# Hybrid encoder, two mixers: Ln/Exp in place of arithmetic roots and softplus, q left unnormalised, the out-projection in three fp32r products, and a new order with other PSUM pools

## The chip, the cores and the metric

The kernel runs on one core of a Trainium2 chip, in one launch. The metric is the device time of an execution in microseconds; the figure given for a kernel is the median of its runs.

## The reference

256 tokens of width 1024 go through two layers. Each layer is FFN, mixer, FFN, all with residuals; a final norm follows. Everything is fp32.

```python
for l in range(DEPTH):                                   # DEPTH = 2
    x = x + 0.5 * swiglu(rms_norm(x, ln_ffn1[l]), ffn1_w_in[l], ffn1_w_out[l])   # D_FF = 2752
    x = x + hybrid_mixer(rms_norm(x, ln_mix[l]), ...)
    x = x + 0.5 * swiglu(rms_norm(x, ln_ffn2[l]), ffn2_w_in[l], ffn2_w_out[l])
return rms_norm(x, ln_final)

def hybrid_mixer(h, ...):
    (wq, wk, wv, dq, dk, dv, dn_qkv, dn_z, dn_beta, dn_a) = split(h @ w_in)
    o_win = window_attention(...)        # 6 heads of 64, 2 kv heads, window 128, sink, ALiBi
    o_d = diff_attention(...)            # 4 heads: softmax(q0 k0) - lam * softmax(q1 k1), ALiBi
    o_diff = rms_norm(o_d, diff_g) * (1 - lam_init)
    qkv = silu(short_conv(dn_qkv, conv_w))               # width 5, 1152 channels
    q = l2_norm(q) * 64 ** -0.5;  k = l2_norm(k)         # rsqrt(sum of squares + EPS)
    beta = sigmoid(dn_beta);  g = -exp(a_log) * softplus(dn_a + dt_bias)
    o_c = gated_delta(q, k, v, beta, g) forwards + backwards   # chunks of 64, triangular solves
    o_dn = rms_norm(o_c, dn_g) * silu(dn_z)
    return concat([o_win, o_diff, o_dn]) @ w_out         # 1024 x 1024
```

## The kernel before

Activations are kept with channels on the 128 partitions: `x` is 128 x 8 x 256, eight channel blocks by 256 tokens. A weight comes as raw fp32 tiles of 128x1024, that is eight blocks of 128x128 (`fetch`, DMA from SP into a pool `rp` of eight buffers).

**The FFNs** multiply in three products. `load` (L243 to L254) makes two fp32r tiles of a raw one: a rounded copy `wh` on ScalarE (L252) and the remainder `wl` on VectorE (L253), both from a pool `wp` with four buffers each. The activations are split in the same way (`xh`, `xl` by `prep`, `hh`, `hl` in `hidden`). `mm3` (L256 to L260) then issues high x high, high x low and low x high for every weight block. 21 hidden blocks and a tail are computed, then eight output blocks. The scale of the norm (`norm_scale`: squares summed over channels with two small matmuls, then `rsqrt`) is applied after the product, in `hidden`, so an FFN starts before its norm is known. The squares are taken by `sq_add`: ScalarE squares a block, GpSimd adds (VectorE in the first FFN).

**The mixers** multiply in fp32: one `matmul` of the program on fp32 operands is two instructions on TensorE. The pieces of a mixer are issued in the order that `ORDER` lists by hand (a piece `name:args` is one call); the framework then schedules each engine's queue from its own model of times, with the place in the program as priority, so instructions can be hoisted over others that wait. The pieces that matter here:

- `A:*`, `N`, `V`, `G`: token projections, the norm, the values and the gates. `G` (`gates`) gets sigmoid and softplus by one Exp and a polynomial on VectorE (L464 to L474).
- `c:a:b`, `co`, `ce`, `qn:a`, `qc`: projection (`proj`, L427) and convolution of nine channel blocks, transposed to tokens; `qn` (`qk_norm`) takes the l2 norm of q (a = 0) and k (a = 1); `qc` transposes them back by chunk.
- `E`, `X`, `i`, `ir`, `im`, `io`, `ie`: decays, products of k and q, and the inverses of 24 triangular matrices, mostly by VectorE multiplies and reductions (`products`, L798 and L799).
- `p:*`, `d:h`, `h:h`, `w:b`, `hw:b`: attention projections, differential scores (`diff_scores`) with a merge of the two softmaxes on GpSimd (L728), window scores, and the heads' outputs.
- `f`, `g`, `sa`, `sb`, `sc`: the rest of the inverse and the scan over four chunks.
- `z`, `ze`, `on:p`: the output gate and the norm of the scan's output (`out_norm`).
- `oT`, `o:part:d`: the three results transposed into `oT`, and the out-projection (`out_proj`, L1047): part 0 uses the channel blocks 0 to 4, part 1 the blocks 5 to 7, eight output blocks each; part 1 ends with `prep` for the next FFN.

PSUM is three pools of banks: `pm` with two, `pd` with four, `pt` with two; `BANK` says which pool a result takes. `SHARED` names operations that go to GpSimd (with ScalarE's help where they start in PSUM). `rsqrt` starts from an integer estimate and takes three Newton steps, eleven VectorE instructions. The two ScalarE functions beyond copies and squares are Exp/Tanh in the mixers and Silu in the FFNs; a change of function table is an instruction on ScalarE (ACT_TABLE_LOAD).

Of the kernel before, what the change touches and what calls it, by code (L numbers as in the profile page):

```python
# [56 lines left out]
class Kernel:  # L57
# [104 lines left out]
    def rsqrt(self, v, n, name, out=None):  # L162

        nc, sp = self.nc, self.sp
        ti = sp.tile([P, n], I32, tag=f"rs_i{n}", name=f"{name}_i")
        nc.vector.tensor_scalar(ti, v.bitcast(I32), 1, None, ALU.arith_shift_right)
        y = sp.tile([P, n], F32, tag=f"rs_y{n}", name=f"{name}_y")
        nc.vector.tensor_scalar(y.bitcast(I32), ti, -1.0, float(0x5F3759DF), ALU.mult, ALU.add)
        a = sp.tile([P, n], F32, tag=f"rs_a{n}", name=f"{name}_a")
        for i in range(3):  # L170
            nc.vector.scalar_tensor_tensor(a, v, -0.5, y, ALU.mult, ALU.mult)
            nc.vector.tensor_tensor(a, a, y, ALU.mult)
            o = y if i < 2 or out is None else out
            nc.vector.scalar_tensor_tensor(o, a, 1.5, y, ALU.add, ALU.mult)
        return o
# [16 lines left out]
    def norm_scale(self, name, last=False):  # L192

        nc = self.nc
        ps = self.psum([P, 512], f"{name}_ps", "pt")
        for p in range(2):
            parts = [t for t in (self.sq, self.sq7) if t is not None]
            for t in parts:
                nc.tensor.matmul(
                    ps[:, p : p + 1], lhsT=t[:, p * P : (p + 1) * P], rhs=self.onec, start=t is parts[0], stop=t is parts[-1]  # L200
                )
# [1 line left out]
        nc.vector.tensor_scalar(v, ps[:, 0:2], 1.0 / D, EPS, ALU.mult, ALU.add)
        rt = self.sp.tile([P, 2], F32, tag="nr", name=f"{name}_r")
        self.rsqrt(v, 2, name, rt)
# [57 lines left out]
    def ffn(self, l, i, gnext, first):  # L263
# [3 lines left out]
        with tc.tile_pool(name=f"hp{nm}", bufs=1) as hp, tc.tile_pool(name=f"ht{nm}", bufs=3) as ht:  # L267
# [18 lines left out]
            late = []  # L286
            for j in range(NF):
# [13 lines left out]
                late.append((j, ps, pu))  # L301
                if j == 1:
                    if first is not None:
                        for k in range(KD):
# [4 lines left out]
                    nc.vector.tensor_scalar(rh, rb, 0.5, None, ALU.mult)
                if j >= 1:  # L310
                    for j_, pg, pu in late:
                        hidden(j_, pg[:, 0:S], pu[:, S : 2 * S], P, (0,))
                    late = []
# [40 lines left out]
    def mixer(self, l, gnext):  # L354
# [22 lines left out]
        with ExitStack() as ctx:  # L377
# [18 lines left out]
            oT = tile_([P, KD, S], "oT")  # L396
# [55 lines left out]
            def gates():  # L452
# [11 lines left out]
                z1 = tile_([P, 2, 24], "z1")  # L464
                ts(z1, ab, 2.0, None, ALU.add)
# [4 lines left out]
                sr = tile_([P, 2, 24], "sr")  # L470
                ts(sr, z2, 2.0 / 17, None, ALU.mult)
                for m in (15, 13, 11, 9, 7, 5, 3):
                    stt(sr, sr, 2.0 / m, z2, ALU.add, ALU.mult)
                stt(sr, sr, 2.0, z1, ALU.add, ALU.mult)  # L474
# [98 lines left out]
            def conv_end(a):  # L573
                if a < 2:
                    st["raw", a] = tile_([P, 2, 384], f"raw{a}", ("t4b", None)[a])
                for p in range(2):
                    act(st["raw", a][:, p, :] if a < 2 else vtok[:, p, :], st["tr", a][p][:, 0:384], AF.Copy)

            def qk_norm(a):

# [4 lines left out]
                nc.vector.tensor_reduce(ss, sqt.rearrange("p t (h d) -> p (t h) d", d=64), AX.X, ALU.add)  # L585
                ts(ss, ss, EPS, None, ALU.add)
                rq = self.rsqrt(ss, 12, f"{nm}qk{a}").rearrange("p (t h) -> p t h", t=2)
                if a == 0:
                    ts(rq, rq, 0.125, None, ALU.mult)
# [153 lines left out]
            def win_out(b):  # L743
# [6 lines left out]
                act(oT[:, b, :], pso[:, 0:S], AF.Copy)  # L750
# [276 lines left out]
            def out_norm(p):  # L1027
# [4 lines left out]
                ts(hv, hv, 1.0 / 64, EPS, ALU.mult, ALU.add)  # L1032
# [8 lines left out]
            def out_proj(part, d):  # L1041
                ks = ((0, 1, 2, 3, 4), (5, 6, 7))[part]
                ps = bank("py")
                for k in ks:
# [2 lines left out]
                    mm(ps[:, 0:S], lhsT=st["o", q // NBLK][:, c], rhs=oT[:, k, :], start=k == ks[0], stop=k == ks[-1])  # L1047
# [58 lines left out]
def build(tc, ins, out, phases=None):  # L1106
    with ExitStack() as ctx:
# [15 lines left out]
        for n, (w, l) in enumerate(order):  # L1123
# [5 lines left out]
            else:  # L1129
                K.ffn(l, int(w[3]), nxt, g(w, l) if n == 0 else None)  # L1130
# [128 lines left out]
```

## Time and profile before

| | |
|---|---|
| time, median of 3 runs | 1138.62 us (1137.33 to 1140.7) |
| the profiled execution | 1140.55 us, of which the trace's span is 1138.8 us |
| mean granted TensorE clock in it | 0.986 |
| FFN 1 of layer 0, from the start | to 198.4 us |
| mixer of layer 0 | 198.4 to 382.5 us |
| FFN 2 of layer 0 and FFN 1 of layer 1 | 382.5 to 755.0 us |
| mixer of layer 1 | 755.0 to 939.8 us |
| FFN 2 of layer 1 and the final norm | 939.8 to 1138.8 us |

Times in the profile are microseconds from the start of the span. PE is TensorE's matmuls, PEld its weight loads, DVE VectorE, ACT ScalarE, POOL GpSimd. A row of a group names line, engine, operation, output and inputs, shapes and count, then busy time and the mean of one in ns. A row of the timeline has start, duration (merged over xN instructions), and in brackets how long the engine sat idle before it and what ended that. A row of the windows has busy time and count for each engine, the granted TensorE clock (PEclk, 1.00 is full speed) and what the DMA moved. Matmuls overlap in the pipeline, so their pace is read from one start to the next and not from the duration of one.

### The profile page before, as it was taken

The page shows a single profiled execution, that of the slowest core. Times are in us where ns is not written, and L with a number is a line of the kernel's source. Part 1 is how long each engine was busy: PE and PEld are TensorE (multiplying, and loading weights), DVE is VectorE, ACT ScalarE, POOL GpSimd, SP SyncE. Part 2 cuts the span into 40 slices and gives each one's busy share as a digit, 9 for nine tenths or more (in the row PEclk, how much of TensorE's full clock was granted, in tenths as well). Part 3 has the DMA queues.
Part 4 walks back from the last instruction along what each step waited for, and adds up shares of the span by engine and source line. Part 5 has one row for each costly group of instructions (what it writes and reads, how often), then busy time and mean ns, then how long its engine had stood idle before and what let it go on. Part 6 is the DMA issues. An engine that isn't in the chain of part 4 may idle for free.

```text
span 1138.8 us, 21945 instructions
## 1 busy us (share of the span) xinstructions
PE 1103.7 (97%) x8970; PEld 1018.8 (89%) x8970; DVE 736.6 (65%) x1434; ACT 523.3 (46%) x967; POOL 75.6 (7%) x127
## 2 busy tenths in 40 slices
PE   7999999988999999999999999999999999999996
PEld 7999999776768999999999999988766789999996
DVE  6766754779847576666566666548796566666653
ACT  6544542263563454544444454424547345445441
POOL 0000011200102100000100000121010020000010
PEclk9999999998999999999999999999988999999998
DMA  8655653421214555565555565533211264556521
GB/s 315 223 185 185 201 182 122 148 93 56 72 42 131 191 178 186 185 200 181 177 182 182 179 201 184 170 121 121 92 56 37 76 204 151 183 184 204 185 94 38
DMA packets 49637, 173.64 MB, mean 152 GB/s; under 512 B 5504, under 2 KB 6784, under 8 KB 49536
## 3 DMA queue, kind: packets, MB, share of 16 engines
q1 hardware_dynamic: 49104, 171.64, 46.2%
q8 instruction: 70, 1.15, 0.4%
q10 hardware_dynamic: 432, 0.60, 0.2%
q14 instruction: 31, 0.25, 0.1%
HBM read 171.17 MB, written 1.05 MB: 151 GB/s over the span
## 4 chain that ended last, share of the span: by engine, by line
PE 80%; DVE 10%; issue 4%; ACT 4%; DMA 1%; POOL 1%; SPq 0%; DVEq 0%; ACTq 0%; POOLq 0%
PE ps L260 21%; PE ps L259 21%; PE ps L258 21%; PE py L1047 5%; PE pj L427 2%; DVE pad L549 2%; PE pz L438 2%; PE pv L438 1%; DVE pr L798 1%; DVE wl L253 1%; PE pso L749 1%; PE pss L712 1%; PE px L968 1%; DMA wr<-in_ffn 1%; DVE mxd L715 1%
## 5 line engine op out<-in xcount | busy, mean ns | idle before, releaser
L253 DVE TENSOR_TENSOR wl<-wr,wh 128x1024 fp32r<-128x1024 f32 x254 | 310.8, 1225 | 175.3 <-ACT wh L252 175.0
L252 ACT ACTIVATE wh<-wr 128x1024 fp32r<-128x1024 f32 x254 | 267.3, 1053 | 249.2 <-issue 143.2
L258 PE MATMUL ps<-xh,wh 128*128 128x256 f32 x1336 | 380.0, 284 | 1.1 <-ACT wh L252 1.1
L260 PE MATMUL ps<-xh,wl 128*128 128x256 f32 x1336 | 379.3, 284 | 0.8 <-DVE wl L253 0.8
L259 PE MATMUL ps<-xl,wh 128*128 128x256 f32 x1336 | 379.1, 284 | 0.0
L258 PEld LDWEIGHTS ps<-xh,wh 128*128 128x128 f32 x1336 | 257.2, 193 | 1.9 <-ACT wh L252 1.3
L260 PEld LDWEIGHTS ps<-xh,wl 128*128 128x128 f32 x1336 | 257.3, 193 | 1.2 <-DVE wl L253 1.2
L259 PEld LDWEIGHTS ps<-xl,wh 128*128 128x128 f32 x1336 | 257.4, 193 | 0.0
L260 PE MATMUL ps<-hh,wl 128*128 128x256 f32 x672 | 188.1, 280 | 0.0
L259 PE MATMUL ps<-hl,wh 128*128 128x256 f32 x672 | 187.9, 280 | 0.0
L258 PE MATMUL ps<-hh,wh 128*128 128x256 f32 x672 | 187.8, 279 | 0.0
L427 PE MATMUL pj<-xf,wr 128*128 128x256 f32 x544 | 130.1, 394 | 2.8 <-issue 2.8
L259 PEld LDWEIGHTS ps<-hl,wh 128*128 128x128 f32 x672 | 126.4, 188 | 0.0
L260 PEld LDWEIGHTS ps<-hh,wl 128*128 128x128 f32 x672 | 126.2, 188 | 0.0
L258 PEld LDWEIGHTS ps<-hh,wh 128*128 128x128 f32 x672 | 126.0, 187 | 0.0
L427 PEld LDWEIGHTS pj<-xf,wr 128*128 128x128 f32 x544 | 105.0, 198 | 19.0 <-issue 3.6
L190 POOL TENSOR_TENSOR sqacc<-sqacc,sqt 128x256 f32<-128x256 f32 x41 | 34.9, 851 | 733.5 <-ACT sqt L186 733.3
L281 ACT ACTIVATE hh<-h 128x256 fp32r<-128x256 f32 x88 | 36.1, 416 | 90.3 <-DVE h L279 90.3
L276 DVE TENSOR_TENSOR t<-ps,f_rb 128x256 f32<-128x256 f32 x88 | 36.8, 423 | 37.7 <-PE ps L260 37.5
L1047 PE MATMUL py<-oT,wr 128*128 128x256 f32 x256 | 57.8, 383 | 0.0
L282 DVE TENSOR_TENSOR hl<-h,hh 128x256 fp32r<-128x256 f32 x88 | 36.8, 423 | 30.5 <-ACT hh L281 30.5
L1047 PEld LDWEIGHTS py<-oT,wr 128*128 128x128 f32 x256 | 47.7, 190 | 6.8 <-DVE x L1054 0.3
(319 smaller groups left out, 1116.4 us busy)
## 6 DMA issues: line engine op xcount, KB each, us to landing
wr<-in_ffn SPq DMA_DIRECT2D x258, 512.0 KB, 3.5
wr<-in_mix SPq DMA_DIRECT2D x50, 512.0 KB, 3.5
wr<-in_mix SPq DMA_DIRECT2D x8, 408.0 KB, 3.1
wr<-in_mix SPq DMA_DIRECT2D x8, 384.0 KB, 3.0
x<-in_x SPq DMA_DIRECT2D x4, 256.0 KB, 4.8
ar<-in_ffn SPq DMA_DIRECT2D x8, 128.0 KB, 4.3
cb<-in_constb SPq DMA_DIRECT2D x1, 588.0 KB, 9.8
out_y<-fo SPq DMA_DIRECT2D x2, 256.0 KB, 2.4
```

The lines of the kernel that those rows point to most:

```text
L190: (eng or nc.gpsimd).tensor_tensor(self.sq, self.sq, t, ALU.add)
L252: nc.scalar.activation(h, w, AF.Copy)
L253: nc.vector.tensor_tensor(lo, w, h.bitcast(F32), ALU.subtract)
L258: mm(out, lhsT=ah, rhs=bh, start=start, stop=False)
L259: mm(out, lhsT=ah, rhs=bl, start=False, stop=False)
L260: mm(out, lhsT=al, rhs=bh, start=False, stop=stop)
L276: nc.vector.tensor_tensor(t[:rows], gate, rb[:rows], ALU.mult)
L281: nc.scalar.activation(hh[:n, j, :], h[:n], AF.Copy)
L282: nc.vector.tensor_tensor(hl[:n, j, :], h[:n], hh[:n, j, :].bitcast(F32), ALU.subtract)
L427: mm(ps[:, 0:S], lhsT=w[:, k * P : (k + 1) * P], rhs=xf[:, k, :], start=k == 0, stop=k == KD - 1)
L438: mm(st[name][p][:, 0:n], lhsT=xf[:, k, p * P : (p + 1) * P], rhs=w[:, c], start=k == 0, stop=k == KD - 1)
L1047: mm(ps[:, 0:S], lhsT=st["o", q // NBLK][:, c], rhs=oT[:, k, :], start=k == ks[0], stop=k == ks[-1])
```

## The change

- `rsqrt` takes Ln and Exp(-0.5 .) on ScalarE and one Newton step on VectorE in the mixers' norm, in `out_norm` and in the final norm (`log=True`); the FFNs' norms, k's norm and the differential norm keep the old form. softplus becomes Ln(1 + Exp(-abs)).
- `log_table` loads the table with Ln and Exp at three places: at a mixer's start, ahead of `on:1`, and in the last FFN.
- q is not normalised: its sum of squares is kept (`qe`), and goes in where `out_norm` had EPS.
- The out-projection multiplies with `mm3`: its weights go through `load` (8 tiles in each mixer), and the heads' outputs are written as `oh` and a remainder `ol` (5 blocks in the buffer of `xl`, 3 in that of k's raw tile).
- The squares for the FFN after a mixer are taken inside that FFN, with VectorE adds, after its second hidden block.
- The score tiles `pss` go from the pool `pm` to `pd`, `pw` from `pd` to `pt`. GpSimd gives up S2, t7 and x0, and gets x6. `ORDER` is changed.

```diff
-A:0 A:1 A:2 K N A:3 G V c:1:0 c:1:1 clear c:0:0 c:1:2 GS co:1:0 c:0:1 co:1:1 co:1:2 ce:1 GE GT E:1 qn:1 co:0:0 co:0:1
-c:0:2 co:0:2 ce:0 qn:0 E:0 E:3 qc:1:1 c:2:0 c:2:1 E:2 qc:0:0 qc:1:0 X:0:0 qc:0:1 ic X:1:1 X:0:1 X:1:0 i ir:1:2 ir:2:3
-ir:3:4 ir:4:5 ir:5:6 p:15 ir:6:7 ir:7:8 im:0 im:1 im:2 c:2:2 im:3 p:14 p:13 co:2:0 p:16 d:0 d:2 co:2:1 io:0 co:2:2 p:9
-d:1 p:12 d:3 w:0 io:1 h:2 h:1 p:10 h:0 io:2 io:3 h:3 p:11 w:1 w:2 hw:0 io:4 io:5 ie ce:2 dn hw:1 f g:0 hw:2 g:1 sa:0
-sb:0 oT:3:4 sc:0 sa:1 sb:1 sc:1 sa:2 sb:2 sc:2 sa:3 sc:3 z:0 z:1 z:2 z:3 ze on:1 o:0:0 on:0 o:0:1 o:0:2 o:0:3 o:0:4
-o:0:5 o:0:6 oT:7 oT:5:6 o:0:7 o:1:0 o:1:1 o:1:2 o:1:3 o:1:4 o:1:5 o:1:6 o:1:7
+lt A:0 A:1 A:2 K N A:3 G V c:1:0 c:1:1 c:0:0 c:0:2 c:1:2 clear GS co:1:0 c:0:1 co:1:1 co:1:2 ce:1 GE GT E:1 qn:1
+co:0:0 co:0:1 co:0:2 ce:0 qn:0 qc:1:1 E:0 E:3 qc:1:0 c:2:0 c:2:1 E:2 qc:0:0 qc:0:1 ic X:0:0 X:1:1 X:0:1 X:1:0 i ir:1:2
+ir:2:3 ir:3:4 ir:4:5 ir:5:6 p:15 ir:6:7 ir:7:8 im:0 im:1 im:2 c:2:2 p:14 p:13 co:2:0 p:16 d:0 d:2 co:2:1 co:2:2 im:3
+io:0 p:9 d:1 p:12 io:1 d:3 w:0 h:2 h:1 p:10 io:2 io:3 io:4 h:3 p:11 w:1 w:2 h:0 hw:0 io:5 ie ce:2 dn hw:1 f g:0 hw:2
+g:1 sa:0 sb:0 oT:3:4 sc:0 sa:1 sb:1 sc:1 sa:2 sc:2 sb:2 sa:3 sc:3 z:0 z:1 z:2 z:3 ze lt on:1 o:0:0 on:0 o:0:1 o:0:2
+o:0:3 o:0:4 oT:7 o:0:5 o:0:6 oT:5:6 o:0:7 o:1:0 o:1:1 o:1:2 o:1:3 o:1:4 o:1:5 o:1:6 o:1:7
...
-    pj="pm", pv="pd", pz="pm", py="pm", pss="pm", ..., po="pd", pw="pd", ...
+    pj="pm", pv="pd", pz="pm", py="pm", pss="pd", ..., po="pd", pw="pt", ...
-SHARED = set("O2 S2 d0 d1 d2 d3 g5 s3 t1 t7 t8 x0 x4 x5".split())
+SHARED = set("O2 d0 d1 d2 d3 g5 s3 t1 t8 x4 x5 x6".split())
...
@@ rsqrt
+        if log:
+            nc.scalar.activation(y, v, AF.Ln)
+            nc.scalar.activation(y, y, AF.Exp, scale=-0.5)
+        else:
...
+        steps = 1 if log else 3
+    def log_table(self):
+        self.tc.keep_in_program_order(self.nc.scalar.preload_act_table_set("natural_log_exp_and_others"))
...
@@ ffn
-                    if first is not None:
+                    if late:
                         for k in range(KD):
                             self.sq_add(k, nc.vector)
...
+            if gnext is None:
+                self.log_table()
...
@@ mixer
-            oT = tile_([P, KD, S], "oT")
+            oh = tile_([P, KD, S], "oh", None, F32R)
+            def ol(k):  # 0..4: buffer of xl; 5..7: buffer of raw1
...
+                if kind == "o":
+                    st[kind, i] = self.load(src, c0, n)
+                    return
...
@@ gates
-                z1 = tile_([P, 2, 24], "z1")
-                ts(z1, ab, 2.0, None, ALU.add)
...
-                for m in (15, 13, 11, 9, 7, 5, 3):
-                    stt(sr, sr, 2.0 / m, z2, ALU.add, ALU.mult)
-                stt(sr, sr, 2.0, z1, ALU.add, ALU.mult)
+                act(sr, ab, AF.Ln, bias=1.0)
...
@@ qk_norm
+                if a == 0:
+                    ts(ss, ss, EPS, 64 * EPS, ALU.add, ALU.mult)
+                    st["qe"] = ss.rearrange("p (t h) -> p t h", t=2)
+                    return
...
@@ win_out, to_oT
-                act(oT[:, b, :], pso[:, 0:S], AF.Copy)
+                act(oh[:, b, :], pso[:, 0:S], AF.Copy)
+                tt(ol(b), pso[:, 0:S], oh[:, b, :].bitcast(F32), ALU.subtract)
...
-                act(oT[:, k0, :], o_, AF.Copy, scale=g)
+                    act(oh[:, k, :], o_, AF.Copy, scale=g)
+                    stt(ol(k), o_, g, oh[:, k, :].bitcast(F32), ALU.mult, ALU.subtract)
...
@@ out_norm, out_proj
-                ts(hv, hv, 1.0 / 64, EPS, ALU.mult, ALU.add)
+                stt(hv, hv, 1.0 / 64, st["qe"][:, p, :], ALU.mult, ALU.add)
...
-                    mm(ps[:, 0:S], lhsT=st["o", q // NBLK][:, c], rhs=oT[:, k, :], start=k == ks[0], stop=k == ks[-1])
+                    wh, wl = st["o", q // NBLK]
+                    self.mm3(ps[:, 0:S], wh[:, c], wl[:, c], oh[:, k, :], ol(k), k == ks[0], k == ks[-1])
...
-                        self.prep(d, gnext)
+                        self.prep(d, gnext, False)
```

More of the change, by code (lines that the diff above doesn't have):

```diff
@@ L47 @@
 BANK = dict(
-    pj="pm", pv="pd", pz="pm", py="pm", pss="pm", pg="pt", pgr="pd", ptr="pd", pkq="pt", pe="pd", pq="pd", p1="pd",
-    p2="pt", pk="pd", px="pt", pS="pt", po="pd", pw="pd", pT="pd", pso="pd", pto="pd",
+    pj="pm", pv="pd", pz="pm", py="pm", pss="pd", pg="pt", pgr="pd", ptr="pd", pkq="pt", pe="pd", pq="pd", p1="pd",
+    p2="pt", pk="pd", px="pt", pS="pt", po="pd", pw="pt", pT="pd", pso="pd", pto="pd",
 )
-SHARED = set("O2 S2 d0 d1 d2 d3 g5 s3 t1 t7 t8 x0 x4 x5".split())
+SHARED = set("O2 d0 d1 d2 d3 g5 s3 t1 t8 x4 x5 x6".split())
 C_M0, C_M1, C_DD, C_WD, C_SEL = 0, 64, 128, 640, 1152
@@ L204, in norm_scale @@
         rt = self.sp.tile([P, 2], F32, tag="nr", name=f"{name}_r")
-        self.rsqrt(v, 2, name, rt)
+        self.rsqrt(v, 2, name, rt, log)
         pb = self.psum([P, 512], f"{name}_pb", "pt")
@@ L260, in mm3, with ffn @@
         mm(out, lhsT=al, rhs=bh, start=False, stop=stop)
-    def ffn(self, l, i, gnext, first):
+    def ffn(self, l, i, gnext, first, late=False):
         nc, tc = self.nc, self.tc
@@ L285, in ffn @@
                 self.start(first, hp, src)
-            late = []
+            wait = []
             for j in range(NF):
@@ L300, in ffn @@
                     self.mm3(o, w[g][0][:, c], w[g][1][:, c], self.xh[:, k, :], self.xl[:, k, :], k == 0, k == KD - 1)
-                late.append((j, ps, pu))
+                wait.append((j, ps, pu))
                 if j == 1:
-                    if first is not None:
+                    if late:
                         for k in range(KD):
@@ L310, in ffn @@
                 if j >= 1:
-                    for j_, pg, pu in late:
+                    for j_, pg, pu in wait:
                         hidden(j_, pg[:, 0:S], pu[:, S : 2 * S], P, (0,))
-                    late = []
+                    wait = []
                 if j == 3 and first is not None:
@@ L395, in mixer @@
             wq = tile_([P, 4, S], "wq")
-            oT = tile_([P, KD, S], "oT")
+            oh = tile_([P, KD, S], "oh", None, F32R)
+            low = {}
+            def ol(k):
+                i = int(k > 4)
+                if i not in low:
+                    low[i] = (
+                        mp.tile([P, 3, S], F32R, tag="raw1", name="olb") if i else
+                        self.xp.tile([P, KD, S], F32R, tag="xl", name="ola")
+                    )
+                return low[i][:, k - 5 * i, :]
             dqk = tile_([P, 2, 2, S], "dqk", "SC")
@@ L574, in conv_end @@
                 if a < 2:
-                    st["raw", a] = tile_([P, 2, 384], f"raw{a}", ("t4b", None)[a])
+                    st["raw", a] = tile_([P, 2, 384], f"raw{a}", ("t4b", "raw1")[a])
                 for p in range(2):
@@ L1129, in build @@
             else:
-                K.ffn(l, int(w[3]), nxt, g(w, l) if n == 0 else None)
+                K.ffn(l, int(w[3]), nxt, g(w, l) if n == 0 else None, n == 0 or order[n - 1][0] == "mix")
         K.final("fin")
```

33 lines of the change are left out of this document (13 added, 20 removed).

## Prediction

> **What bounds the kernel now.** I read the page's engine totals first, then windows by stage, then windows of 10 us inside a mixer, then the timelines where TensorE or VectorE stood idle. From the page:
>
> ```profile
> span 1138.8 us, 21945 instructions
> PE 1103.7 (97%) x8970; PEld 1018.8 (89%) x8970; DVE 736.6 (65%) x1434; ACT 523.3 (46%) x967; POOL 75.6 (7%) x127
> ...
> L253 DVE TENSOR_TENSOR wl<-wr,wh 128x1024 fp32r<-128x1024 f32 x254 | 310.8, 1225 | 175.3 <-ACT wh L252 175.0
> L252 ACT ACTIVATE wh<-wr 128x1024 fp32r<-128x1024 f32 x254 | 267.3, 1053 | 249.2 <-issue 143.2
> ...
> L276 DVE TENSOR_TENSOR t<-ps,f_rb 128x256 f32<-128x256 f32 x88 | 36.8, 423 | 37.7 <-PE ps L260 37.5
> ```
>
> 97% for PE looks like a matmul bound everywhere. The windows by stage say otherwise: the FFNs have no idle PE, the mixers some.
>
> ```profile
> 382.50:755.00 372.50, 372.30 (x3121) 371.89 (x3121) 231.19 (x336) 170.80 (x242) 13.05 (x15) 1.00 0.56 179
> 755.00:939.80 184.80, 177.43 (x1362) 135.79 (x1360) 131.97 (x355) 87.63 (x234) 24.30 (x39) 0.96 0.31 101
> ```
>
> Columns after the length: PE, PEld, DVE, ACT, POOL with counts, then the granted clock, DMA share, GB/s. A mixer is not one thing either. Windows inside the mixers:
>
> ```profile
> 278.40:288.40 10.00, 10.00 (x33) 6.67 (x32) 7.72 (x14) 4.39 (x16) 2.52 (x2) 0.74 0.17 54
> ...
> 825.00:835.00 10.00, 8.17 (x32) 4.79 (x30) 9.79 (x17) 3.82 (x14) 0.00 (x0) 0.91 0.22 70
> 835.00:845.00 10.00, 10.00 (x34) 7.05 (x34) 7.69 (x14) 4.16 (x13) 2.53 (x2) 0.75 0.18 53
> 845.00:855.00 10.00, 9.29 (x43) 6.64 (x42) 9.96 (x14) 5.06 (x18) 1.27 (x1) 0.93 0.20 54
> 855.00:865.00 10.00, 10.00 (x41) 8.27 (x40) 8.35 (x14) 5.02 (x17) 2.49 (x1) 0.73 0.08 24
> ...
> 915.00:925.00 10.00, 10.00 (x48) 8.80 (x48) 8.12 (x26) 4.22 (x6) 1.50 (x1) 1.00 0.63 194
> 925.00:935.00 10.00, 10.00 (x51) 8.86 (x50) 5.36 (x10) 4.55 (x10) 2.23 (x2) 1.00 0.87 303
> ```
>
> In the middle (inverse and scores) DVE is full at 9.79 and 9.96 of 10, and the TensorE clock is granted at 0.73 to 0.75 for stretches, in which DVE idles 2.28, 2.31 and 1.65 us. In the last third (915 to 935, the out-projection) PE is full at clock 1.00 and DVE and ACT are not: TensorE time saved there counts in full.
>
> **Out-projection.** Timelines of PE, and of the queue that feeds its second part:
>
> ```profile
> 183.12 0.28 PE L258 MATMUL ps<-hh,wh 128*128 128x256 f32 x1
> ...
> 190.54 0.28 PE L343 MATMUL ps<-hh,th 128*128 128x256 f32 x1
> ...
> 927.16 12.72 PE L1047 MATMUL py<-oT,wr 128*128 128x256 f32 x58
> ```
> ```profile
> 357.33 11.85 PE py L1047 x54
> 369.19 0.66 PE pto L411 x6
> ```
> ```profile
> 364.01 0.56 DVE L1036 TENSOR_TENSOR O<-zt,m0on_y 128x384 f32<-128x384 f32 x1
> ```
>
> A weight block costs two fp32 instructions, 2 x 12.72/58 = 0.438 us. In an FFN 63 fp32r matmuls start between 183.12 and 190.54, 0.118 us each, so `mm3` costs 0.353 us. 64 blocks x 0.085 = 5.4 us a mixer, 10.9 us in both. It adds, per mixer, 8 copies of 1.05 us on ACT and 8 remainders of 1.225 us on DVE, and 8 remainders of `ol` at about 0.42 us (row L276, same shape, from PSUM). Where they lie: four buffers of `wp` are free through the mixer, so four tiles can be split early; the other four follow in the out-projection, where today's four splits for the next FFN stand, and those move later, to the FFN's pace. DVE holds 13.5 us in the 20 us to 935; with 2 more splits (2.5) and three `ol` (1.3), less what `rsqrt` saves, it needs about 16 of 17 us. That fits narrowly, and the chain to part 1 narrows as well: the last normalised output ends at 364.57 and PE asks for it at 369.19, 4.6 us of slack. 27 blocks that are 0.085 shorter take 2.3, and `oT:5:6` now has one output of five blocks less ahead of it at issue, 1.8 if the schedule follows. Some 0.5 is left, 1 more from the shorter `rsqrt`; one extra split of 1.225 is covered, two are not. I charge 0.75 us per mixer (ends 0 and 2.5): 1.5.
>
> **Softplus, q and the norms.** The chain of waits, then the timelines:
>
> ```profile
> 211.33 0.20 DVE z L465
> ...
> 214.21 0.21 DVE sr L473
> ```
> ```profile
> 229.94 0.53 PE L411 MATMUL ptr<-cst,cs 128*128 128x128 f32 x2 [1.17 <-DVE cs L570]
> 249.45 0.84 PE L411 MATMUL pkq<-cst,raw 128*128 128x128 f32 x6 [0.89 <-DVE raw L592]
> 785.82 0.53 PE L411 MATMUL ptr<-cst,cs 128*128 128x128 f32 x2 [0.49 <-DVE cs L570]
> ```
> ```profile
> 244.49 0.17 DVE L166 TENSOR_SCALAR m0qk_i<-ss 128x12 int32<-128x12 int32 x1
> 248.47 0.17 DVE L589 TENSOR_SCALAR m0qk_y<-m0qk_y 128x12 f32<-128x12 f32 x1
> 248.75 1.02 DVE L592 TENSOR_TENSOR raw<-raw,m0qk_y 128x384 f32<-128x384 f32 x2
> ```
>
> The polynomial is 12 DVE steps in a row, 211.33 to 214.41; one Ln replaces it, so about 2.8 us of DVE and latency go. q's norm is 12 small steps strung from 244.49 to 248.64 (about 2.1 us of work, between others) and two multiplies, 1.02. PE is otherwise full in this stretch, so what can come back is what PE waited: 1.17 + 0.89 in layer 0, 0.49 + 0.89 in layer 1 (I take 0.89 there too, the k and q pieces being the same). Softplus addresses the first, q's norm the second: 3.4 us, and about 1 more since `qc:1:0`, k's, now stands ahead of `c:2:0` and leaves fewer copies in front of `X`. I take 4.0, ends 2 and 7.
>
> **The DVE-bound middle.** The list of waits and the timeline:
>
> ```profile
> PE pss L707 <- ACT sc L718: 3.0, 2, 1.5
> ```
> ```profile
> 831.47 0.38 PE L707 MATMUL pss<-ddb,sdiag 128*128 128x512 bf16 x1 [1.52 <-ACT sc L718]
> ```
>
> Once per mixer PE waits 1.5 us for a score bank, and within 2 us the clock falls (0.75 in 835 to 845), which starves DVE. With scores in four banks, and projections alone in `pm`, that wait should go. The DVE idle tied to low clock is 2.28 in layer 0 and 2.31 + 1.65 in layer 1, 6.2 in all; I take half, 3.1 (ends 0 and 6.2, plus PE time in the rival below). Against it: splits of the first out-projection tiles can be queued between the inverse's steps. Two per mixer would cost 4 x 1.225 = 4.9; I take half, 2.5, for those that fall into gaps (ends 0 and 9.8, all four early ones in the way). The order's moves (merges next to `io`, `im:3` later) I price at nothing: same instructions, and DVE has to execute all.
>
> **Tables, squares, the end.** ACT, then the chain of waits:
>
> ```profile
> 200.04 1.28 ACT L459 ACT_TABLE_LOAD   x1
> 201.34 0.21 ACT L459 ACTIVATE ea<-row 128x12 f32<-128x12 f32 x1
> ```
> ```profile
> 1128.88 0.18 DVE fin_i L166
> ...
> 1130.85 0.17 DVE fin_r L174
> ```
> ```profile
> 394.44 0.16 DVE L203 TENSOR_SCALAR f_v<-f_ps 128x2 f32<-128x2 f32 x1 [1.02 <-PE f_ps L199]
> ```
>
> A load costs 1.30 us from its start to the next ACT instruction. `lt` at a mixer's start takes the place of this one; I count one more for the first Tanh and one ahead of `on:1`, and one at the end: 5 x 1.3 = 6.5 us on ACT. It is more than half idle at the out-projection (4.22 and 4.55 of 10) and in a mixer as a whole (87.63 of 184.80), so nothing on the path; uncovered, 6.5. S2 and t7 come back from GpSimd to DVE, two steps of about the 0.51 that L592's take, where PE is full: nothing, at most 2 in both mixers.
>
> What ACT_TABLE_LOAD costs is also stated by the Trainium skill (ScalarE: Activation LUTs, section "What ACT_TABLE_LOAD costs"): 1283 ns and a drain of about 1380 ns, 2.66 us for a switch. The load's own 1.28 agrees; the drain does not show, ACT going on 0.02 us after it. By the page five loads are an estimated 13.3 us of ACT, which its idle time would still hold.
>
> Squares after a mixer: the FFN's norm scale is first read at 394.44, 12 us after the FFN began, and PE runs ahead meanwhile; eight squares and seven DVE adds (0.42 each) fit, cost nothing; if not covered 3 us each time, 6. The final `rsqrt` is bare at the end: 11 steps, 1128.88 to 1131.02, 2.1 us; two small ACT steps and three DVE steps at 0.2 each, with hand-overs, are 1.2. Gain 0.9.
>
> **Sum.** 10.9 - 1.5 + 4.0 + 3.1 - 2.5 + 0.9 = 14.9 us off the profiled execution's 1140.55 (span 1138.8 and 1.75 around it): 1125.6. The median shown, 1138.62, is 1.9 lower, so I predict 1123.7.
>
> **Rivals** (times at the level of the median; a change within 0.3%, 3.4 us, can hardly be told from none here).
>
> *Pool of four becomes the bound (slower).* `pd` now holds the pair `pss`, the pair `ptr` until `ce:2`, `pT`, `pso`: six wanted, four there. Each mixer has 7 score groups and 7 head outputs that can wait, on a PE queue that holds up all behind it. At 1.52 us each, as in the row above, 5 waits a mixer eat the gain; with one per score group, 7, it is 21.3 us in both mixers, and the time 1145. Against it: with two banks shared with projections, scores waited only once per mixer.
>
> *The splits sit in the inverse.* All four early ones delay DVE (9.8 in place of 2.5) and the clock stays as it is (minus 3.1): gain 4.5, 1134. For it: DVE is at 9.96. Against: ACT must copy first, and there are DVE gaps after 865 (8.35 of 10 and less).
>
> *The clock is no longer cut.* Low clock costs PE the missing share: in the quoted windows 2.6, 0.9, 2.5, 0.7 and 2.7 us, 9.4 together. If that and all the idle DVE time come back, 3.1 + 7 or so on top: 1113. For it: fewer PE gaps. Against: other gaps remain.
>
> On this the Trainium skill (TensorE: Matmul & The Clock Gate, "Part 1: The HAM clock gate", under "What's actually happening") says that the clock goes to half after at least one idle window of about 3.4 us. Here it falls after a gap of 1.52, so the trace disagrees. By that rule a wait of that length would have no hold on the clock, the 3.1 us in the sum would be nothing, and the time 1126.8.
>
> *It does not do what it says:* the fp32r pairs arrive too late and PE waits for each, so that the out-projection gains nothing: 1123.7 + 10.9 = 1135.
>
> **How the numbers follow.** Forecast 0.56, splits in the inverse 0.15, clock 0.16, pool of four 0.10, late pairs 0.03. Faster by over 0.3%: 0.56 + 0.16 and 0.10 of the 0.18 in the two weak gains, 0.82; within: 0.08; slower: 0.10. The forecast alone spans 1116 to 1132 from the ends above; to leave out two in ten the range takes in the weak gains above and most of the clock case below: 1111 to 1137.
>
> **What would show it.** Right: L1047's rows gone, L258 to L260 grown by 128 each, and out-projection windows at PE 10.00 that are some 5 us shorter; no `pss` wait on ACT sc; `pkq` not waiting for `raw`; a PEclk above 0.96 in the mixers. Wrong: PE rows of the out-projection waiting for `wl` or `ol`; `pss`, `pT` or `pso` waiting for ACT; DVE remainders L253 among L798 and L799; PE idle at the start of FFN 2.

## The result: 1138.0 to 1121.8 us, and the profile after

The kernel after takes 1121.82 us (median of 4, 1121.02 to 1122.8) against 1137.98 (median of 4) for the kernel before beside it: ratio 0.9852, 95% interval 0.9833 to 0.9871. The profiled execution took 1121.32 us. That of before, 1140.55, lies 2.6 us over its median, so the two profiles differ by more (19.3 us of span) than the medians (16.2). The page of after, and its windows by stage with the row that the prediction left out for before (columns as there):

```profile
span 1119.5 us, 22207 instructions
PE 1077.2 (96%) x9098; PEld 1009.7 (90%) x9098; DVE 751.0 (67%) x1374; ACT 545.4 (49%) x1006; POOL 60.1 (5%) x109
```
```profile
198.43:382.31 183.88, 174.62 (x1361) 133.24 (x1360) 133.69 (x355) 87.42 (x234) 24.32 (x47) 0.98 0.32 101
```
```profile
197.57:371.77 174.20, 161.39 (x1425) 128.56 (x1424) 137.01 (x322) 95.99 (x249) 18.47 (x40) 0.98 0.32 104
371.77:746.77 375.00, 374.69 (x3122) 374.32 (x3121) 234.86 (x345) 172.72 (x244) 11.50 (x13) 1.00 0.55 179
746.77:920.95 174.18, 161.70 (x1426) 128.74 (x1424) 136.90 (x322) 95.96 (x249) 18.10 (x32) 0.98 0.31 104
```

The mixers lost 9.7 and 10.6 us (183.9 and 184.8 to 174.2 and 174.2). The two FFNs between them, in which the change touches only where squares are taken, grew from 372.67 (382.31 to 754.98) to 375.00. A mixer is best cut at the first step after the inverses (`f`, the first `p<-WA`): before and after, layer 0.

```profile
328.33 1.61 PE L928 MATMUL p<-WA,XE 32*32 32x32 f32 x96
```
```profile
323.20 1.61 PE L955 MATMUL p<-WA,XE 32*32 32x32 f32 x96
```

From the mixer's start that is 129.9 and 125.6 us; from there to the FFN 54.0 and 48.6. So 4.3 us come from the part up to `f` and 5.4 from the part with the scan and the out-projection. What stands just ahead of `f` shows in the chain of waits (start, us, engine, tile and line), first of before, then of after:

```profile
305.47 0.41 ACT sc L698
...
317.86 2.20 PE pz L438 x6
...
321.67 2.58 PE pz L438 x8
...
325.26 2.13 PE pz L438 x6
```
```profile
309.80 1.14 DVE wl L265
...
311.10 0.68 ACT sc L723 x2
...
320.54 0.63 ACT hn L791
...
323.27 1.54 PE p L955 x94
```

Ahead of `f` the chain runs over ScalarE (window softmax, copies of heads and of the inverse's blocks) in both kernels, from 305.5 and from 311.1. In before its last 10 us, from 317.9, lie on PE, with 6.9 us of the output gate's projection `pz`; after, these have run earlier. The windows say the same: ahead of `f` ScalarE is full for 20 us, in the last ten of them PE is nearly full too in before (9.74), and VectorE is not.

```profile
297.60:307.60 10.00, 8.70 (x44) 7.19 (x44) 9.94 (x17) 5.90 (x22) 2.54 (x1) 1.00 0.17 52
307.60:317.60 10.00, 8.50 (x49) 6.37 (x49) 6.42 (x16) 9.87 (x24) 0.00 (x0) 1.00 0.17 52
317.60:327.60 10.00, 9.74 (x40) 5.18 (x42) 3.81 (x17) 9.10 (x27) 0.00 (x0) 1.00 0.05 9
```
```profile
307.60:317.60 10.00, 9.23 (x48) 6.30 (x49) 6.45 (x21) 9.89 (x34) 0.00 (x0) 1.00 0.44 159
317.60:327.60 10.00, 9.38 (x187) 6.02 (x187) 5.00 (x20) 9.13 (x17) 0.00 (x0) 1.00 0.35 109
357.60:367.60 10.00, 8.64 (x71) 8.18 (x70) 8.38 (x14) 6.35 (x13) 1.44 (x3) 1.00 0.47 154
283.50:290.30 6.80, 4.09 (x13) 3.11 (x14) 6.80 (x10) 3.86 (x10) 1.26 (x1) 0.50 0.28 77
```

The first fence is before, the second after. Its last two rows: in the out-projection PE is at 8.64 of 10, no longer full, and the clock is still halved once a mixer. The waits of after (us in all, times, longest), and three of the four early splits, on VectorE:

```profile
PE pss L699 <- DVE c L748: 11.3, 2, 5.8
...
PE py L270 <- DVE x L1082: 1.8, 4, 0.6
```
```profile
284.45 1.22 DVE L265 TENSOR_TENSOR wl<-wr,wh 128x1024 fp32r<-128x1024 f32 x1
...
290.33 1.21 DVE L265 TENSOR_TENSOR wl<-wr,wh 128x1024 fp32r<-128x1024 f32 x1
...
292.89 1.21 DVE L265 TENSOR_TENSOR wl<-wr,wh 128x1024 fp32r<-128x1024 f32 x1
```

The score wait on ScalarE is gone; in its place PE waits up to 5.8 us once a mixer for VectorE. As far as VectorE bounds this stretch, the wait costs nothing itself: VectorE is busy for 5.74 of its 5.77 us, and for 6.80 of 6.80 in the halved stretch that begins inside it.

### The profile page after: what moved, and what is told of

It is laid out like the page before. It is cut to its first block, busy times and chain, and to the rows that moved or that the text cites. A ratio compares the mean times of both kernels' runs of the same rounds, so it can differ in the third digit from the quotient of the medians.

```text
span 1119.5 us, 22207 instructions
## 1 busy us (share of the span) xinstructions
PE 1077.2 (96%) x9098; PEld 1009.7 (90%) x9098; DVE 751.0 (67%) x1374; ACT 545.4 (49%) x1006; POOL 60.1 (5%) x109
## 4 chain that ended last, share of the span: by engine, by line
PE 78%; DVE 13%; ACT 4%; issue 3%; DMA 1%; POOL 1%; DVEq 0%; SPq 0%; ACTq 0%
PE ps L272 21%; PE ps L270 21%; PE ps L271 21%; PE pj L455 4%; PE pv L466 2%; DVE pr L825 2%; DVE wl L265 2%; PE py L270 1%; DVE pp L826 1%; PE py L271 1%; PE py L272 1%; DVE pad L568 1%; ACT wh L264 1%; DVE mxd L740 1%; PE px L995 1%
## 5 line engine op out<-in xcount | busy, mean ns | idle before, releaser
L265 DVE TENSOR_TENSOR wl<-wr,wh 128x1024 fp32r<-128x1024 f32 x270 | 330.5, 1226 | 167.6 <-ACT wh L264 167.1
L264 ACT ACTIVATE wh<-wr 128x1024 fp32r<-128x1024 f32 x270 | 284.2, 1054 | 243.9 <-issue 153.0
L270 PE MATMUL ps<-hh,wh 128*128 128x256 f32 x672 | 190.2, 283 | 0.0
L270 PEld LDWEIGHTS ps<-hh,wh 128*128 128x128 f32 x672 | 129.0, 192 | 0.0
L271 PEld LDWEIGHTS ps<-hl,wh 128*128 128x128 f32 x672 | 129.0, 192 | 0.0
L272 PEld LDWEIGHTS ps<-hh,wl 128*128 128x128 f32 x672 | 129.0, 192 | 0.0
L455 PEld LDWEIGHTS pj<-xf,wr 128*128 128x128 f32 x544 | 101.7, 193 | 18.3 <-issue 3.9
L198 POOL TENSOR_TENSOR sqacc<-sqacc,sqt 128x256 f32<-128x256 f32 x27 | 24.5, 907 | 741.6 <-ACT sqt L194 741.6
L194 ACT ACTIVATE sqt<-x 128x256 f32<-128x256 f32 x49 | 19.8, 409 | 56.3 <-DVE x L361 52.5
L568 DVE SCALAR_TENSOR_TENSOR pad<-pad,cwh 128x256 f32<-128x256 f32 x68 | 33.1, 487 | 12.1 <-ACT pad L562 6.8
```

What stands on the lines that cost most here:

```text
L198: (eng or nc.gpsimd).tensor_tensor(self.sq, self.sq, t, ALU.add)
L264: nc.scalar.activation(h, w, AF.Copy)
L265: nc.vector.tensor_tensor(lo, w, h.bitcast(F32), ALU.subtract)
L270: mm(out, lhsT=ah, rhs=bh, start=start, stop=False)
L271: mm(out, lhsT=ah, rhs=bl, start=False, stop=False)
L272: mm(out, lhsT=al, rhs=bh, start=False, stop=stop)
```

## The experiments

Medians against the kernel before on the same chip (1138.0 to 1139.1 us). "To `f`" and "to the FFN" are the two parts of a mixer in the profiled execution, the second up to the FFN's first product behind the last one of the out-projection.

| kernel | us | ratio, 95% interval | layer 0: to `f`, to the FFN | layer 1 |
|---|---|---|---|---|
| before | | 1 | 129.9, 54.0 | 130.8, 54.0 |
| before + split out-projection | 1146.08 | 1.0053 (1.0034 to 1.0071) | 132.2, 52.7 | 134.6, 53.5 |
| the same + short root, squares moved | 1140.54 | 1.0008 (0.9997 to 1.0019) | 131.4, 50.8 | 134.7, 51.9 |
| before + order and pools | 1128.55 | 0.9910 (0.9893 to 0.9926) | 123.9, 53.1 | 124.7, 52.9 |
| after | 1121.82 | 0.9852 (0.9833 to 0.9871) | 125.6, 48.6 | 125.7, 48.5 |
| after, out-projection in fp32 | 1127.04 | 0.9890 (0.9867 to 0.9914) | 124.0, 52.8 | 124.7, 52.7 |
| after, squares back | 1125.25 | 0.9872 (0.9854 to 0.9889) | 125.8, 49.7 | 124.9, 49.8 |
| after, polynomial and q's norm back | 1135.67 | 0.9951 (0.9929 to 0.9972) | 127.1, 55.3 | 125.9, 55.3 |
| after, pools back | 1144.84 | 1.0053 (1.0033 to 1.0074) | 134.8, 51.5 | 133.4, 51.5 |

**The split out-projection, alone and taken out**

```diff
 # before, with
+st["o", i] = self.load(src, c0, n)
+self.mm3(ps[:, 0:S], wh[:, c], wl[:, c], oh[:, k, :], ol(k), k == ks[0], k == ks[-1])
 # after, with
-self.mm3(...)
+mm(ps[:, 0:S], lhsT=st["o", q // NBLK][:, c], rhs=oT[:, k, :], ...)
```

> The kernel before with one part of the change alone: the out-projection in three fp32r products (weights through load, heads' outputs as oh and a remainder ol). Order, pools, softplus, roots and q stay as before. Theory A (the parts add up): 64 blocks a mixer at 0.353 in place of 0.438 us are 5.4 us a mixer, and the stretch from the last px to the FFN shrinks from 27.1 to about 21.6 us in each mixer; time about 10 us under before (0.991). Rival B (the gain needs the other parts: without the new order and the shorter rsqrt the split tiles and ol come late, or the splits sit in the inverse): PE waits for wl or ol in the out-projection, or the inverse ends later, and the time is less than 5 us under before (over 0.9956).

> The kernel after with the out-projection taken back to fp32 (raw weights, oT), all else as after. Theory A: 5.4 us a mixer come back at the out-projection, and the splits no longer lie among the inverse's steps, so what is lost is 10.8 us less what these cost (3 x 1.22 a mixer at most): 4 to 11 us over after, 1126 to 1133. Rival B (splits in the inverse cost as much as they bring, and the gain of the change is in the rest): within 3 us of after.

Alone, it makes the kernel slower; rival B held by its time and by the later inverse (the waits for `wl` or `ol` that it named did not come). Windows of its mixers and its longest wait of PE in the out-projection, then the mixer and `f` of after in fp32:

```profile
196.33:381.18 184.85, 174.62 (x1428) 134.90 (x1426) 142.31 (x369) 94.30 (x242) 23.36 (x47) 0.97 0.30 98
754.42:942.46 188.04, 177.87 (x1427) 136.99 (x1426) 141.92 (x369) 94.19 (x242) 23.21 (x39) 0.95 0.31 96
```
```profile
PE py L258 <- DVE x L1071: 5.2, 6, 1.3
```
```profile
197.23:374.04 176.81, 166.14 (x1362) 128.95 (x1360) 128.42 (x311) 89.90 (x242) 17.62 (x40) 0.98 0.33 105
```
```profile
321.22 1.61 PE L940 MATMUL p<-WA,XE 32*32 32x32 f32 x96
```

In before's order the splits push `f` back by 2.3 and 3.8 us, and PE then waits for VectorE's sums into `x` (5.2 us in both mixers), so that only 1.3 and 0.5 of the 5.4 us a mixer come through. In after the same edit is worth 5.2 us: `f` comes 1.6 and 1.0 us later, and the part behind it is 4.2 us shorter in each mixer. Theory A held there.

**Two parts that make room at the end**

```diff
 # before + split out-projection, with
+r = self.rsqrt(hv, 6, f"{nm}on{p}", log=True)     # lt ahead of on:1
+self.prep(d, gnext, False)                        # squares inside the FFN
 # after, with
-self.prep(d, gnext, False)
+self.prep(d, gnext)
```

> The kernel before with the split out-projection, and two more parts of the change: the rsqrt of out_norm by Ln and Exp with one Newton step (with the table load ahead of on:1), and the squares after a mixer taken inside the FFN. 64 unused bytes keep hh and hl at the addresses of before. The split alone measured 1146.1 us, 7 over before: off1 came 2.3 and 3.8 us later in the mixers, and the stretch from the last px to the FFN stayed at 27 us although the products are 5.4 us shorter. Theory A (the end of a mixer is bound by the chain of small VectorE steps to oT:5:6 and by ScalarE and VectorE work on x, xh, squares and splits, so that shorter products pay only with these taken out): the stretch falls to 22 us or less, 5 us a mixer under the split alone, about 1136, and off1 stays as late as in the split alone. Rival B (the split weights themselves come late, by DMA or for want of buffers): the stretch stays at 26 us or more, time about 1145.

> The kernel after with the squares after a mixer back at the mixer's end (eight ScalarE squares of 0.40 us between the xh, adds on GpSimd), all else as after. Theory A: in the split out-projection's end ScalarE then has 3.2 us more among the xh and the splits of the next FFN, PE waits, and 2 to 3 us a mixer are lost: 1126 to 1128. Rival B (ScalarE has room, as the prediction had it for the move): within 1.5 us of after, 1121.8.

With both parts added to the split alone, the stretch from the last px to the FFN fell from 27 to 25.1 us, not to 22: A only by half, B wrong. The time is that of before. The squares alone, put back into after, cost 3.4 us, just under what A had and twice what B allowed.

**Order and pools**

```diff
 # before, with the new ORDER (without lt), BANK and SHARED
 # after, with
-pss="pd", pw="pt"
+pss="pm", pw="pd"
```

> The kernel before with the new order, the new pools (pss in pd, pw in pt) and the new list of GpSimd's operations, and nothing else of the change (fp32 out-projection, polynomial, q normalised, Newton roots, squares at the mixer's end). Alone, the split out-projection was 7 us slower than before; taking the pools out of after cost 23 us, the early arithmetic 14, the split 5. Theory A (order and pools are what makes the room: they take out the score waits, after which the clock is cut and VectorE starves, and let z and the out-projection run under the inverse): off1 earlier than 129.9 by 2 us or more per mixer, 4 to 8 us under before, 1131 to 1135. Rival B (each part only pays with the others; with VectorE as full as in before, the order gives nothing): within 3.4 us of before, 1136 to 1142.

> The kernel after with the pools back (pss in pm, pw in pd), the new order and all else as after. Theory A (the middle is bound by VectorE; where the scores wait matters little): last window score later, off1 within 1 us of after, time within 2 us of after, 1120 to 1124. Rival B (the score waits and the clock cut behind them held VectorE, the prediction's 3.1 us): off1 1.5 us later or more in each mixer, time 1125 or more.

Order and pools (with the new list of GpSimd's operations, which was not run apart) alone bring 10 us, more than A had it. A's mechanism is not what shows, though: PE's wait for a score bank, 1.5 us in before, stays.

```profile
PE pss L707 <- ACT sc L718: 2.9, 2, 1.4
```

Only the halved clock behind it is shorter: the granted clock of layer 0 is 0.90 and 0.93 in the two windows of 10 us from 267.6, where before has 0.96 and 0.70. With the new pools the wait is gone only where VectorE's early work is gone as well (after, and after in fp32); with the polynomial and q's norm back in after it is 1.5 us again, with the old pools 1.8. The mixers of this run, a stretch ahead of `f`, and `f`; then the last window scores in before, here, and in after with the pools back:

```profile
198.45:375.51 177.06, 166.38 (x1362) 128.00 (x1360) 132.03 (x357) 86.59 (x233) 22.50 (x45) 0.99 0.33 105
748.26:925.87 177.61, 167.75 (x1362) 129.14 (x1360) 131.81 (x357) 86.95 (x233) 22.18 (x37) 0.98 0.33 105
```
```profile
297.60:307.60 10.00, 9.77 (x53) 6.70 (x53) 9.45 (x21) 8.94 (x23) 0.01 (x1) 1.00 0.33 105
```
```profile
322.39 1.61 PE L928 MATMUL p<-WA,XE 32*32 32x32 f32 x96
```
```profile
313.90 1.66 PE L674 MATMUL pss<-wq 64*128 64x256 f32 x8
```
```profile
303.70 1.14 PE L674 MATMUL pss<-wq 64*128 64x256 f32 x8
```
```profile
319.35 1.13 PE L699 MATMUL pss<-wq 64*128 64x256 f32 x4
```

The last window scores come 10 us earlier, ScalarE's softmax work is taken up earlier (8.94 of 10 in the window from 297.6, where before has 5.90), and `f` comes 6 us earlier. That each follows from the one before it is read from the traces; no run holds the scores back alone. With the pools back, the new order is worse than the old, and B held by more than it asked: `f` is 9.2 and 7.7 us later than in after. PE waits 1.61 us for VectorE and, 5 us on, 1.66 for a score bank, and a stretch of 13.7 us at half clock lies there, in which VectorE is busy for 9.81 only.

```profile
269.40 0.38 PE L732 MATMUL pss<-ddb,sdiag 128*128 128x512 bf16 x1 [1.61 <-DVE dqk L686]
...
274.48 0.58 PE L732 MATMUL pss<-ddb,sdiag 128*128 128x512 bf16 x1 [1.66 <-ACT sc L743]
```
```profile
269.70:283.40 13.70, 11.62 (x29) 7.16 (x29) 9.81 (x15) 5.53 (x20) 1.26 (x1) 0.50 0.00 1
```

So the new order needs the pools; whether they would bring as much in the old order was not run.

**Softplus and q**

```diff
 # after, with
-act(sr, ab, AF.Ln, bias=1.0)
+...                                   # the polynomial
-if a == 0: st["qe"] = ...; return     # q's sum of squares kept
+rq = self.rsqrt(ss, 12, ..., log=False); ts(rq, rq, 0.125, ...); two multiplies
```

> The kernel after with the polynomial for softplus and the normalisation of q (rsqrt in three Newton steps, two multiplies) back, out_norm with EPS; order, pools, split out-projection and out_norm's Ln and Exp as after. Theory A (all VectorE work ahead of the inverse delays it one for one, since VectorE is full from there to off1): about 2.8 us of polynomial and 3.1 us of q's norm come back on VectorE, pq and off1 come 3 to 5 us later in each mixer, time 6 to 10 us over after, 1128 to 1132. Rival B (only PE's own waits come back, as the prediction counted, 4.0 in both mixers): about 1125.8, off1 later by 2 us a mixer.

Both theories missed the place. The inverse starts 2.4 us later in both mixers (first multiply `pr` 61.8 us into the mixer, 59.4 in after), but `f` only 1.5 and 0.2 us; the time is lost behind it. PE idles 3.08 us ahead of `f`, and the clock is then halved for 17.1 us in each mixer:

```profile
323.73 1.11 PE L781 MATMUL pso<-PT,V 128*64 128x256 f32 x2 [3.08 <-ACT PT L772]
```
```profile
323.10:340.20 17.10, 16.47 (x264) 12.50 (x266) 7.18 (x24) 8.01 (x16) 0.00 (x0) 0.50 0.02 5
```

The runs lie between 1128.8 and 1137.8, and their granted clock goes along, from 0.986 in the fastest to 0.976 in the slowest; the two fastest, 7 us over after, fall into A's range. Only the profiled one (1136.53, clock 0.978) shows where its time went. In the other direction the parts bring next to nothing: from "before + order and pools" to "after, out-projection in fp32" (which adds softplus, q, roots and squares) the mixers go from 177.06 and 177.61 to 176.81 and 177.42. Their granted clock falls with it, from 0.99 and 0.98 to 0.98 and 0.96, so part of what these parts save may go there; no run separates it.

**The FFN's pace.** In after 63 products on hh take 7.56 us (189.77 to 197.33), 0.1200 each; in before it was 0.118. The groups of all four FFNs (before, after; busy us, mean ns):

```profile
L258 PE MATMUL ps<-hh,wh 128*128 128x256 f32 x672 | 187.8, 279 | 0.0
```
```profile
L270 PE MATMUL ps<-hh,wh 128*128 128x256 f32 x672 | 190.2, 283 | 0.0
```

2016 products by 0.0022 us are 4.4 us. With `log=True` the two small integer tiles of out_norm's root are gone, and hh and hl stand 64 bytes lower in SBUF. Measured from a multiple of 512 bytes, the weight tiles and xh, xl start at 480 in both kernels, hh and hl at 32 in before and at 480 in after.

```diff
 # after, with unused tiles: 64 bytes ahead of hh; 64, 32, 256 ahead of x; 32 ahead of all
+nc.vector.memset(self.sp.tile([P, 16], F32, tag="pad", name="pad64", bufs=1), 0.0)
+pad = self.rp.tile([P, 16], F32, tag="pad", name="pad", bufs=1)     # 8, 64
+nc.vector.memset(cp.tile([P, 8], F32, name="pad"), 0.0)
```

> The kernel after with 64 bytes per partition of unused space ahead of the FFN's pool, so that hh and hl stand at the addresses that they have in before (after, they stand 64 bytes lower); the heads' oh moves by 64 too, nothing else. Theory A (the place of the moving operand in SBUF sets the pace of the fp32r products): the 2016 products on hh and hl return from 0.1200 to 0.1178 us each, the two middle FFNs from 375.0 to 372.7 us, and the time is 4.4 us under after (about 1117.4, 0.996). Rival B (the pace differs by chip or by execution, or comes from the weights): pace and time as after, 1121.8, within 1 us.

> As the run with 64 bytes ahead of the FFN's pool, but the 64 bytes stand ahead of x, xh, xl and all that follows, the weights' tiles staying where they are. Then xh and xl have the same offset within 1024 bytes as hh and hl in before. Theory A: the 4008 products on xh and xl speed up too, from 0.1200 to 0.1178 us, 8.8 us more: about 13 us under after (1108.6, 0.988). Rival B (chip or execution): as after. Rival C (the address matters, but it is that of hh against that of xh or the weights, not the offset): a gain of 4.4 or none, xh staying at 0.120.

> The kernel after with 32 unused bytes per partition ahead of x, so that xh, xl, hh, hl start on a multiple of 512 bytes; the weights stay at 480 past one. So far: moving operand at 480 past a multiple of 512, 0.1200 us a product; at 32 past it, 0.1178, and in one FFN of the profiled run 0.1133. Theory A (the address of the moving operand in SBUF decides, and a read that starts 32 bytes short of a 512-byte line is the slow one): 0.1178 or less, time 1089 to 1109. Theory B (the distance between weights and moving operand decides, 0 slow and 64 fast): half the distance, so somewhere between, 1100 to 1122, and not below the run with 64 bytes.

> The kernel after with 32 unused bytes ahead of all weight tiles and activations: weights, xh, xl, hh and hl all start on a multiple of 512 bytes, their distances as in after. Theory A (address of the moving operand): as with 32 bytes ahead of x alone, 0.1178 or less, 1089 to 1109. Theory B (distance between weights and moving operand): 0.1200 as in after, 1121.8. If the weights' own start matters too, the weight loads (192 ns in after, 188 in before on hh) get shorter and the pace falls below 0.1178.

> The kernel after with 256 unused bytes per partition ahead of x: the moving operands start 256 bytes from the weights' offset within 512. So far, by this distance: 0 (after, and all tiles moved together by 32) 0.1200 us a product, 32 0.1168, 64 0.1178 with stretches of 0.1133. If the distance within 512 bytes decides, farthest is at least as good as 64: 0.1178 or less everywhere, and 0.1133 in more of the FFNs if the pull towards the slow pace weakens with distance: 1080 to 1102. If it were the absolute address (the read starting 32 short of a line), 224 past a multiple of 512 would give 0.1178 or less as well, but that reading already failed with all tiles moved together. If the effect comes back every 128 or 256 bytes: 0.1200 and 1121.

| unused bytes | distance from the weights' offset: xh, hh | us | ratio, 95% interval | us a product: xh, hh |
|---|---|---|---|---|
| none (after) | 0, 0 | 1121.82 | 0.9852 (0.9833 to 0.9871) | 0.1200, 0.1200 |
| 64 ahead of hh | 0, 64 | 1116.57 | 0.9796 (0.9773 to 0.9818) | 0.1200, 0.1178 |
| 64 ahead of x | 64, 64 | 1096.51 | 0.9625 (0.9591 to 0.9659) | 0.1178, 0.1178; one FFN 0.1133 |
| 32 ahead of x | 32, 32 | 1102.77 | 0.9689 (0.9669 to 0.9709) | 0.1168, 0.1168 |
| 32 ahead of all | 0, 0 | 1121.58 | 0.9856 (0.9838 to 0.9875) | 0.1200, 0.1200 |
| 256 ahead of x | 256, 256 | 1122.62 | 0.9861 (0.9844 to 0.9879) | 0.1200, 0.1200 |

The pace of a stretch can be read from one window row, length by count of PE's instructions: the two middle FFNs with 64 bytes ahead of hh, a stretch of the second and one of the third FFN with 64 ahead of x, the two FFNs with 32 ahead of x, with 32 ahead of all, and with 256.

```profile
370.47:743.12 372.65, 372.34 (x3122) 371.96 (x3121) 234.63 (x345) 172.75 (x244) 11.50 (x13) 1.00 0.56 180
```
```profile
368.66:555.00 186.34, 186.09 (x1581) 185.92 (x1580) 122.81 (x182) 92.65 (x132) 5.05 (x7) 1.00 0.58 187
575.00:715.00 140.00, 140.00 (x1237) 140.00 (x1236) 92.60 (x127) 68.87 (x98) 3.64 (x4) 1.00 0.59 193
```
```profile
366.69:731.80 365.11, 364.66 (x3122) 364.28 (x3121) 234.76 (x345) 172.69 (x244) 11.49 (x13) 1.00 0.58 184
```
```profile
371.49:746.50 375.01, 374.71 (x3123) 374.33 (x3122) 234.80 (x345) 172.71 (x244) 11.48 (x13) 1.00 0.55 179
```
```profile
371.00:746.00 375.00, 374.70 (x3122) 374.32 (x3122) 234.78 (x345) 172.68 (x244) 11.49 (x13) 1.00 0.55 179
```

140.00 by 1237 is 0.113; 365.11 by 3122 is 0.117; 375.00 by 3122 is 0.120. In before, with 0 and 64, xh and hh go at 0.1200 and 0.1178. Moving all tiles together changes nothing, moving the activations against the weights does: what counts is the distance, not the address (B of the run with all moved; with 32 ahead of x alone the activations start at the same offset as there and are fast). The pace does not go evenly with the distance, as B of the run with 32 ahead of x had it: 0.1168 at 32 is below 0.1178 at 64.

The gain that was expected at 256 bytes did not come; the slow pace is back there. Against a period of 128 bytes stands that the remainders `ol` of blocks 5 to 7, which start 384 bytes from the weights' offset in the two runs with 64 bytes, go at 0.115 in the out-projection (median from start to start, 24 a mixer); a period of 256 was not tested further.

With 64 bytes ahead of hh theory A held (1116.57 for 1117.4); with 64 ahead of x, xh and xl follow as A had it, and stretches at 0.1133 take the time 12 us below A's 1108.6. The six runs with 64 bytes lie near 1102, 1096 and 1089, steps of about 6.7 us; an FFN with 1,500 products at 0.1133 in place of 0.1178 saves 6.8, so one, two or three FFNs at the fast pace would fit, though only one execution was profiled. What makes an FFN fall into the fast pace is open. The run with 64 bytes ahead of x is the best version: 43 us under before.

## Why the prediction was right, and where not

The time, 1123.7 forecast and 1121.8 measured, was right by terms that were not, and that is luck: order and pools brought 10.9 us more than their term, the early arithmetic 3.6 less, and the FFN's pace, which no term holds, took 4.4. In the order of its steps:

- **Out-projection, 10.9 less 1.5 for the tail: nearly right.** Against after in fp32 the part behind `f` is 4.2 us shorter in each mixer, 8.4, so 2.5 of the 10.9 are missing in place of 1.5. About 1.5 of these are pace and not tail: most products of the out-projection go at 0.120 in after, like its FFNs, and an fp32 instruction takes 0.216 us from start to start where the prediction divided a length that ends with the last instruction's end (0.219). That leaves about 1.0 for the tail. The named mechanism is there: the last normalised output ends later than PE asks for it, and an extra split stands in its chain.

```profile
355.30 1.23 DVE L265 TENSOR_TENSOR wl<-wr,wh 128x1024 fp32r<-128x1024 f32 x1 [0.19 <-ACT wh L264]
...
358.35 0.56 DVE L1063 TENSOR_TENSOR O<-zt,m0on_y 128x384 f32<-128x384 f32 x1
```
```profile
358.96 0.44 PE L436 MATMUL pto<-cst,O 128*128 128x128 f32 x2 [0.97 <-DVE O L1063]
```

- **Splits in the middle, 2.5: right,** 1.6 and 1.0 us. Three of the four early ones stand among the inverse's steps, the fourth in the chain of waits at 309.80.
- **Softplus and q, 4.0: wrong.** The step counted what PE had waited early on and took that as gain at the mixer's end. The inverse does begin earlier, 59.3 us into the mixer in after in fp32 and 62.7 with order and pools alone, more than the 2.0 a mixer of this step. But the path ahead of `f` goes over ScalarE, full for 20 us at 9.87 and 9.10 of 10 in before. The prediction's windows stopped short of these rows, and it took ScalarE as idle from the mixer's mean. The runs show 0.4 us for both mixers with the other arithmetic parts. Taken out of after, the two cost 14 (7 to 16 from run to run), by another way: a longer wait on ScalarE and a halved clock. That ScalarE is what took the head start is read from the windows, not tested by a run.
- **Score banks and clock, 3.1 with ends 0 and 6.2: mis-sized, and the largest miss.** Order and pools alone take 6.8 and 7.2 us off the mixers, 14.0. The step's mechanism was wrong as well: four banks do not take the wait away (1.4 us there, once a mixer), and its bound was the VectorE time that PE's low clock had idled. By the traces, what pays is that scores and the gate's projection run earlier and ScalarE's stretch begins earlier. The sentence that priced "the order's moves" at nothing is the one that failed.
- **Squares, nothing: right for where they went, and blind for where they left.** Put back, they cost 3.4 us.
- **Tables, nothing:** after has five loads more, as counted (11 for 6); no run shows what they cost by themselves.
- **Final root, 0.9: right.** From `fin_v` to `fin_r` it takes 1.06 us (1111.16 to 1112.22) in place of 2.14: 1.1.

```profile
1111.00 0.16 DVE L215 TENSOR_SCALAR fin_v<-fin_ps 128x2 f32<-128x2 f32 x1 [1.43 <-PE fin_ps L211]
...
1112.06 0.16 DVE L182 SCALAR_TENSOR_TENSOR fin_r<-fin_a,fin_y 128x2 f32<-128x2 f32 x1
```

- **Not in the sum: the FFN's pace,** 4.4 us the wrong way, from 64 bytes of layout.

By the profiled spans: 14.0 (order and pools), 0.4 (arithmetic), 5.8 (split, net), 1.3 (first and last FFN) less 2.3 (middle FFNs) is 19.2 of 19.3 us; the shares hold for this sequence of runs, since a part brings more or less by what it is added to.

Of the signs named, the waits went as said (no `pss` on ACT, no `pkq` on `raw`), and PEclk is 0.98 in both mixers, which that of layer 0 had before as well; PE at 10.00 in the out-projection did not come (8.64). Of the rivals, the pool of four did not become the bound; in the new order the old pools are the slower ones. "Late pairs" did not happen: no `py` waits for `wl` or `ol`. "The clock is no longer cut" was right for half of layer 1's share: the clock is halved for 6.8 us in each mixer of after, under full VectorE, and for 6.8 and 13.7 us in before. The Trainium skill (TensorE: Matmul & The Clock Gate, "Part 1: The HAM clock gate", under "What's actually happening") gives windows of 3413 ns; the halved stretches here, 6.8, 13.7 and 17.1 us, are two, four and five of these. That it takes an idle window of that length first the traces do not bear out: waits of 1.61 and 1.66 us stand at the start of the 13.7 us and 5 us on.

## What to carry to other kernels

Measure parts of a change in both directions: alone the split cost 7 us, and in company it brought 5; the parts taken out of after cost 5, 3, 14 and 23 us, 45 in all, for a change that brought 16, so no part has a price of its own. Ahead of any gain look for the engine that is full between the place of the saving and the end, stretch by stretch up to the last row, and not at means. When a stage that was not touched changes its pace, look at what moved in SBUF.

## What was not expected of the hardware

- The pace of 256-column fp32r products depends on where the moving operand lies against the weights: 0.1200 us at distances of 0 and 256 bytes (from the same offset within 512), 0.1168 at 32, 0.1178 and at times 0.1133 at 64. By this alone the same program goes from 1121.8 to 1096.5 us.
- How long the clock stays halved did not go by PE's waits at the start of it: 13.7 us with waits of 1.61 and 1.66 us, 17.1 us with one of 3.08, 6.8 us with one of 5.8. What sets the length is open.
